# Two projection stages of a hybrid decoder block, ordered by hand, with the last two row blocks by column halves

## The chip, the cores and the metric

The kernel runs on one core of one Trainium2 chip. The metric is the device time of one execution in microseconds, as the median of several runs; a profiled execution gives the trace. The engines are PE (matmul, with its weight loads PEld beside it), DVE (vector), ACT (activation), POOL (GpSimd) and SP, which here only issues DMA.

## The reference

A decoder block (one layer, 256 rows of width 1024, fp32) with two parallel token mixers, a gated MLP and a final norm. Only its start concerns the change: the modulation from c, the norm, and the one wide input projection that feeds both mixers.

```python
cond = jax.nn.silu(c)
mod = (cond @ ada_w[layer] + ada_b[layer])[:, None, :]
shift_m, scale_m, gate_m, shift_f, scale_f, gate_f = jnp.split(mod, 6, axis=-1)
h = rmsnorm(x, norm_mix_g[layer]) * (1.0 + scale_m) + shift_m
...
p = split_columns(h @ w_in)   # q, k, v of the sparse attention, gates, latents, merge gates
...
o_nsa = lax.map(lambda a: nsa_one(*a, rel_table), (q, kc, vc, ks, vs, kw, vw, gates))
o_mla = mla_attention(p["mla_cq"], p["mla_ckv"], p["mla_krope"], ...)
y = jax.nn.sigmoid(p["merge_a"]) * o_nsa + jax.nn.sigmoid(p["merge_b"]) * o_mla
x = x + gate_m * (y @ w_o)
...
x = x + gate_f * conv_glu_ffn(h, ...)
return rmsnorm(x, final_norm_g)
```

Inside `nsa_one` every logit gets a bias from a small table by the distance of query and key.

## The kernel before

**Splitting.** Every fp32 operand is kept as two fp32r parts, hi and lo = value − hi. A product is three matmuls, hi·hi, hi·lo and lo·hi (`mm3`, L178). For a weight, ACT makes hi (L135) and DVE makes lo (L136) from the loaded tile `raw`. For the modulated input, tile by tile of 128 columns, DVE makes `hf` (L397), ACT its hi part `hh` (L398), DVE its lo part `hl` (L402).

**The start.** The transposed input xT comes in four loads on SP's queue; the parameters `par` and the identity (a part of `cst`) on ACT's. Eight matmuls broadcast silu(c) along the partitions into `crow`, which ACT copies out of PSUM (L300). Squares of xT (ACT, L304) are added up on DVE (L311) and reduced over partitions by matmuls with `ones` (L221); ACT and POOL make the inverse root, DVE scales the identity by it into `sq` (L268), and one matmul with ones broadcasts it (L272, `rsp`). `busy(n)` (L282) issues n matmuls of `ones` by `ones`, which compute nothing that is used; `WARM` holds how many stand at three places.

**Stage 1** (L410) multiplies eight row blocks k of `wA` (1024 × 2048), each in two column halves of eight tiles, into all eight PSUM banks: tags lg, lg, pt, pt, o, mm, mm, ms, called accA. A block is 48 matmuls of 128x256. The column of the modulation that block k + 1 needs is made meanwhile (`modulate`, L384): two rows of `adaA` are loaded, and DVE takes two dot products with `crow` (`gemv`, L377), then `am` (L393) and `mod` (L395).

**Stage 2** (L504) multiplies eight blocks of `wvg` (1024 × 560, 12 matmuls of 128x280 each) into the banks lg, lg, pt, pt, which must be emptied first: `t_evac` (L462 on ACT or L464 on DVE, as `TE` says) takes the lg banks, and `k_evac` the pt banks, as a copy on ACT (L478) and a subtraction on DVE (L479) from the same bank. `q_evac` (L448, L449) does the same for o, mm, mm, ms, which the attention's first logits need. At the end ACT copies v (L518) and the gates (L519) out.

**What sets the order.** A scheduler orders the instructions of each engine by the priorities of `prio` and by the code's order; `EV` orders the evacuations. `prefetch` keeps up to three weights loaded and split ahead. SP's queue takes the loads in the scheduler's order; each waits until the buffer it writes is free. The four loads of `BT` (L426, 512 KB each) read the table of biases from DRAM, shifted by partition. `tables` (L327) makes cosine and sine on DVE, from positions and the rest of `cst`.

**After stage 2** come the attention of both mixers with further projections between (list `WORK`), the output projection, the gated MLP and the last norm.

Of the kernel before, what the change touches and what calls it, by code (L numbers as in the profile page):

```python
# [14 lines left out]
AX = mybir.AxisListType  # L15

# [16 lines left out]
C_ID, C_MASK, C_VM, C_ROWV, C_IF, C_SGN = 0, 128, 512, 520, 521, 522  # L33
N_CST = 523

N_A = 16
WARM = (6, 3, 4)
# [3 lines left out]
HB = 3  # L41
# [5 lines left out]
EV = "k1 q1 t0 q3 q2 k0 d q0 t1"  # L47
# [3 lines left out]
TE = "avvvaaav"  # L51
# [4 lines left out]
def body(tc, a, out, dbg=None):  # L56
    nc = tc.nc
    with ExitStack() as ctx:
# [79 lines left out]

        depth = [3]
# [151 lines left out]
        acc = xsq[:, 0, :]  # L291
# [3 lines left out]
        with tc.issue_after(last[-1]):  # L295
            for c in range(2):
                ps = bank("pt")
                for i in range(4):
                    mm(ps[:, i * 128:i * 128 + 128], free(cond[:, 4 * c + i:4 * c + i + 1], [[0, 128]]), ident, True, True)
                nc.scalar.activation(crow[:, c * 512:c * 512 + 512], ps[:], AF.Copy)  # L300
        with tc.issue_after(silu), tc.issue_after(half):
            for i in range(4):
                sq = xsq.t[i // 2][:, i % 2 * 2:i % 2 * 2 + 2, :]
                nc.scalar.activation(sq, xT.t[i // 2][:, i % 2 * 2:i % 2 * 2 + 2, :], AF.Square)  # L304
                for j in range(2):
                    if i == 3 and j == 0:
                        ssq.reduce(acc, True, False)
                    if i == 3:
                        last.append(ssq.reduce(sq[:, j, :], False, j == 1))
                    elif i + j > 0:  # L310
                        nc.vector.tensor_tensor(acc, acc, sq[:, j, :], ALU.add)  # L311
# [15 lines left out]
        def tables():  # L327
# [6 lines left out]
            nc.sync.dma_start(cst[:, 128:], a["cst"][:, 128:])  # L334
# [47 lines left out]
        nc.vector.tensor_scalar(sb1[:], par[:, C_ADAB + 8:C_ADAB + 16], 1.0, None, ALU.add)  # L382

        def modulate(k):  # L384
            for j in (1, 0):
                if k % 3 < 2:
                    ad = l4(F32, [128, 1024])
                else:
                    ad = st.tile([128, 1024], F32, tag="ad", name=nm("ad"), bufs=2)
                nc.sync.dma_start(ad[:], a["adaA"][k, :, j])  # L390
                gemv(mod[:, 8 * j + k:8 * j + k + 1], ad[:])
# [3 lines left out]
            nc.vector.tensor_tensor(mod[:, k:k + 1], mod[:, k:k + 1], par[:, C_ADAB + k:C_ADAB + k + 1], ALU.add)  # L395
            hf = t1("hf")
            nc.vector.scalar_tensor_tensor(hf[:], xT[:, k, :], am[:], rst[:] if k else rsp, ALU.mult, ALU.mult)  # L397
            h0 = nc.scalar.activation(hh[:, k, :], hf[:], AF.Identity, bias=mod[:, k:k + 1]).ins  # L398
            if k == 0:
                with tc.issue_after(h0):  # L400
                    nc.scalar.activation(rst[:], rsp, AF.Copy)
            nc.vector.scalar_tensor_tensor(hl[:, k, :], hf[:], mod[:, k:k + 1], hh[:, k, :], ALU.add, ALU.subtract)  # L402

        modulate(0)
        nc.vector.tensor_scalar(vec[:], psv[0:16, 0:384], -1.0, None, ALU.mult)
        nc.gpsimd.dma_start(vdr[:], vec[:])
        prefetch(2)
        accA = [bank(t) for t in ("lg", "lg", "pt", "pt", "o", "mm", "mm", "ms")]
        prefetch(2)
        for k in range(8):  # L410
            if k < 7:
                modulate(k + 1)
            prefetch(3)
# [781 lines left out]
```

## Time and profile before

| | before |
|---|---|
| median of 3 runs | 456.95 us (456.25 to 459.64) |
| the profiled execution | 458.63 us, span 456.8 us |
| busy share of the span: PE, PEld | 96%, 91% |
| DVE, ACT, POOL | 80%, 62%, 6% |
| mean granted TensorE clock | 0.992 |

The span is the time from the first to the last instruction in the trace of one execution; the execution's own time lies 1.8 us above it. A busy share is the mean over stages with different limits, so the stages are looked at one by one. In a row of a timeline the bracket gives the idle time of the engine ahead of the instruction and what ended it; rows with "xN" hold N records that follow one another. Durations overlap where an engine is pipelined.

### The profile page before, as it was taken

The page shows a single profiled execution, that of the slowest core. Times are in us where ns is not written, and L with a number is a line of the kernel's source. Part 1 is how long each engine was busy: PE and PEld are TensorE (multiplying, and loading weights), DVE is VectorE, ACT ScalarE, POOL GpSimd, SP SyncE. Part 2 cuts the span into 40 slices and gives each one's busy share as a digit, 9 for nine tenths or more (in the row PEclk, how much of TensorE's full clock was granted, in tenths as well). Part 3 has the DMA queues.
Part 4 walks back from the last instruction along what each step waited for, and adds up shares of the span by engine and source line. Part 5 has one row for each costly group of instructions (what it writes and reads, how often), then busy time and mean ns, then how long its engine had stood idle before and what let it go on. Part 6 is the DMA issues. An engine that isn't in the chain of part 4 may idle for free.

```text
span 456.8 us, 9366 instructions
## 1 busy us (share of the span) xinstructions
PE 439.2 (96%) x3514; PEld 414.5 (91%) x3514; DVE 366.5 (80%) x873; ACT 282.3 (62%) x610; POOL 26.2 (6%) x45
## 2 busy tenths in 40 slices
PE   6999989999989999999999999999999999999994
PEld 6899978777869879999989999999999999999993
DVE  3899988878788878899989888778778778778643
ACT  4444475879698996656657776556556556546332
POOL 1100042030010111000000000000000000000001
PEclk9899999999999999999999999999999999999998
DMA  7999898779762337997857875655655655653002
GB/s 279 414 406 377 252 311 238 290 269 297 261 213 95 101 121 250 305 317 254 296 206 220 252 259 189 194 179 178 193 185 168 199 187 165 204 187 93 1 0 93
DMA packets 31565, 99.33 MB, mean 217 GB/s; under 512 B 4293, under 2 KB 6933, under 8 KB 31520
## 3 DMA queue, kind: packets, MB, share of 16 engines
q1 hardware_dynamic: 30208, 96.59, 62.7%
q0 software_dynamic: 1024, 1.98, 1.9%
q8 instruction: 28, 0.46, 0.4%
q10 hardware_dynamic: 288, 0.17, 0.2%
q14 instruction: 17, 0.14, 0.1%
HBM read 96.01 MB, written 1.14 MB: 213 GB/s over the span
## 4 chain that ended last, share of the span: by engine, by line
PE 79%; DVE 6%; DMA 6%; ACT 4%; issue 2%; POOL 1%; DVEq 0%; POOLq 0%; SPq 0%; ACTq 0%
PE mm L176 29%; PE lg L176 12%; PE o L176 12%; PE ms L176 11%; PE pt L176 10%; DMA ad<-in_adaR 3%; DMA cst<-in_cst 2%; PE pt L860 2%; DVE lo L136 2%; DVE ad L377 1%; ACT hi L135 1%; ACT pt L864 1%; PE ms L221 1%; ACT s L608 0%; DVE s L449 0%
## 5 line engine op out<-in xcount | busy, mean ns | idle before, releaser
L176 PE MATMUL mm<-s,hi 128*128 128x256 f32 x552 | 105.2, 288 | 0.6 <-DVE s L991 0.3
L136 DVE TENSOR_TENSOR s<-raw,s 128x1024 fp32r<-128x1024 f32 x66 | 80.5, 1221 | 17.9 <-PE mm L176 14.5
L176 PE MATMUL mm<-s,s 128*128 128x258 f32 (+1 forms) x544 | 94.1, 283 | 0.0
L176 PEld LDWEIGHTS mm<-s,hi 128*128 128x128 f32 x552 | 85.3, 189 | 3.7 <-issue 1.2
L135 ACT ACTIVATE s<-raw 128x1024 fp32r<-128x1024 f32 x66 | 69.0, 1051 | 23.2 <-PE mm L176 23.2
L176 PEld LDWEIGHTS mm<-s,s 128*128 128x128 f32 x544 | 77.6, 189 | 0.1
L176 PE MATMUL mm<-s,lo 128*128 128x256 f32 x268 | 76.9, 287 | 0.1
L136 DVE TENSOR_TENSOR lo<-raw,hi 128x1024 fp32r<-128x1024 f32 (+2 forms) x55 | 63.5, 1161 | 5.6 <-ACT hi L135 5.4
L135 ACT ACTIVATE hi<-raw 128x1024 fp32r<-128x1024 f32 (+2 forms) x55 | 53.5, 989 | 21.0 <-PE mm L176 6.8
L176 PEld LDWEIGHTS mm<-s,lo 128*128 128x128 f32 x268 | 50.5, 188 | 1.5 <-issue 0.7
L176 PE MATMUL o<-s,s 128*128 128x258 f32 (+1 forms) x272 | 47.8, 283 | 0.0
L377 DVE CUSTOM_DVE_ANT_0 ad<-ad,crow 128x1024 f32<-128x1024 f32 x36 | 43.6, 1218 | 3.2 <-DMA ad<-in_adaR 2.9
L176 PE MATMUL ms<-s,s 128*128 128x258 f32 x264 | 46.1, 283 | 0.0
L176 PEld LDWEIGHTS o<-s,s 128*128 128x128 f32 x272 | 39.0, 189 | 0.0
L176 PEld LDWEIGHTS ms<-s,s 128*128 128x128 f32 x264 | 37.7, 189 | 0.0
L176 PE MATMUL lg<-zh,s 128*128 128x256 f32 x176 | 34.7, 280 | 0.0
L176 PE MATMUL pt<-zh,s 128*128 128x256 f32 x176 | 34.6, 279 | 0.0
L839 ACT ACTIVATE L<-L,sm 128x128 f32<-128x128 f32 (+1 forms) x64 | 28.3, 449 | 1.4 <-DVE sm L835 1.4
L176 PEld LDWEIGHTS lg<-zh,s 128*128 128x128 f32 x176 | 28.6, 188 | 0.0
L176 PEld LDWEIGHTS pt<-zh,s 128*128 128x128 f32 x176 | 28.5, 188 | 0.0
L835 DVE CUSTOM_DVE_ANT_0 L<-lg,s 128x128 f32<-128x128 f32 (+1 forms) x64 | 20.9, 350 | 8.6 <-PE lg L176 8.0
L176 PE MATMUL lg<-s,s 128*128 128x256 f32 (+4 forms) x104 | 27.3, 350 | 0.5 <-DVE sm L835 0.5
(250 smaller groups left out, 810.4 us busy)
## 6 DMA issues: line engine op xcount, KB each, us to landing
ad<-in_adaR SPq DMA_DIRECT2D x32, 512.0 KB, 4.6
raw<-in_wg SPq DMA_DIRECT2D x22, 512.0 KB, 3.5
raw<-in_wu SPq DMA_DIRECT2D x22, 512.0 KB, 4.4
raw<-in_wd SPq DMA_DIRECT2D x22, 512.0 KB, 4.5
raw<-in_wA SPq DMA_DIRECT2D x16, 512.0 KB, 8.0
raw<-in_wm SPq DMA_DIRECT2D x16, 512.0 KB, 4.9
L<-in_adaA SPq DMA_DIRECT2D x12, 512.0 KB, 7.9
raw<-in_cw SPq DMA_DIRECT2D x8, 512.0 KB, 5.3
```

What stands on the lines that cost most here:

```text
L135: nc.scalar.activation(hi[:], raw[:], AF.Copy)
L136: nc.vector.tensor_tensor(lo[:], raw[:], hi[:], ALU.subtract)
L176: nc.tensor.matmul(o, l, r, start=start, stop=stop, **kw)
L221: m = nc.tensor.matmul(self.ps[:, tt:tt + 1], sq[:, tt * 128:tt * 128 + 128], ones[:, 0:1], start=first and tt == 0, stop=last, skip_group ...
L377: nc.vector.tensor_tensor_reduce(out=ad, in0=ad, in1=crow[:], scale=1.0, scalar=0.0, op0=ALU.mult, op1=ALU.add, accum_out=dst)
L835: nc.vector.tensor_tensor_reduce(out=L[:, br, j, 0:nk], in0=lgj[:, br, :], in1=bias_view(2 * t + j, qt), scale=1.0, scalar=3e38, op0=ALU.a ...
L839: nc.scalar.activation(L[:, br, j, 0:nk], L[:, br, j, 0:nk], AF.Exp, scale=-1.0, bias=sm[:, i:i + 1], accum_out=sm[:, 4 + i:5 + i])
L860: nc.tensor.transpose(pt[:, (kb * 2 + j) * 128:(kb * 2 + j) * 128 + 128], self.L[qt][:, br, j, kb * 128:kb * 128 + 128], ident)
L864: nc.scalar.activation(self.PT[qt, br][:, 0:qt + 1, :], pt[:, 0:(qt + 1) * 256].rearrange("p (b q) -> p b q", b=qt + 1), AF.Copy)
```

## The change

1. **Order by hand.** Stages 1 and 2, from the first `modulate` to the gates, stand in `tc.manual_schedule` for DVE, ACT and PE: these engines take them in the order of the code. `prefetch` is split for it into `fetch` (the load), `head` (hi) and `rest` (lo).
2. **Column halves.** The weights of `wA` come as before for blocks 0 to 5, then (6, half 0), (7, half 0), (6, half 1), (7, half 1). After the second of these the banks lg and pt are complete: `k_evac(1)`, `t_evac(0)`, `k_evac(0)` and `t_evac(1)` stand beside the other two, all eight copies of `t_evac` on ACT. `q_evac` is issued one half bank per block of stage 2. Stage 2 takes the row halves in the order 1, 0.
3. **The start.** The identity is a part of `par` and comes with it in one load on SP; xT comes in two loads on ACT's queue. DVE copies `crow`, ACT scales the identity, ACT makes `am` and `mod` and the negated `vec`; POOL prepares `sb1`. Each half of the squares is reduced by itself, and ones-matmuls stand at four places. Block 0 issues its products as all hi·hi, then hi·lo, then lo·hi.
4. **Around it.** `BT` is written behind stage 1; `tables` and the first later `gemv` wait for the gates' last instructions.

```diff
-WARM = (6, 3, 4)
+WARM = (5, 3, 3, 2)
-EV = "k1 q1 t0 q3 q2 k0 d q0 t1"
-TE = "avvvaaav"
+TE = "aaaaaaaa"
...
-        for k in range(8):
-            for c in range(2):
-                plan(a["wA"][k, :, c * (N_A // 2) * 128:(c + 1) * (N_A // 2) * 128], N_A // 2 * 128)
+        for k, c in [(k, c) for k in range(6) for c in range(2)] + [(6, 0), (7, 0), (6, 1), (7, 1)]:
+            plan(a["wA"][k, :, c * 1024:c * 1024 + 1024], 1024)
...
-        nc.scalar.dma_start(par[:], a["par"])
-        nc.scalar.dma_start(ident, a["cst"][:, C_ID:C_ID + 128])
-        for i in range(4):
-            nc.sync.dma_start(xT.t[i // 2][:, i % 2 * 2:i % 2 * 2 + 2, :], a["xT"][:, 2 * i:2 * i + 2, :])
+        ident = par[:, N_PAR:N_PAR + 128]
+        nc.sync.dma_start(par[:], a["par"])
+        for i in range(2):
+            nc.scalar.dma_start(xT.t[i][:], a["xT"][:, 4 * i:4 * i + 4, :])
...
+        for h in range(2):
+            t = xsq.t[h]
+            for j in range(2):
+                nc.vector.tensor_tensor(t[:, 2 * j, :], t[:, 2 * j, :], t[:, 2 * j + 1, :], ALU.add)
+            with tc.issue_after(last[-1]):
+                last.append(ssq.reduce(t[:, 0, :], h == 0, False))
+            with tc.issue_after(last[-1]):
+                last.append(ssq.reduce(t[:, 2, :], False, h == 1))
+            busy(WARM[2])
...
-            nc.vector.scalar_tensor_tensor(am[:], mod[:, 8 + k:9 + k], sb1[:, k:k + 1],
-                                           par[:, C_GMIX + k:C_GMIX + k + 1], ALU.add, ALU.mult)
+            nc.scalar.activation(am[:], mod[:, 8 + k:9 + k], AF.Identity, scale=par[:, C_GMIX + k:C_GMIX + k + 1],
+                                 bias=sb1[:, k:k + 1])
+            nc.scalar.activation(mod[:, k:k + 1], mod[:, k:k + 1], AF.Identity, bias=par[:, C_ADAB + k:C_ADAB + k + 1])
...
+        with tc.manual_schedule(engines={EN.DVE, EN.Activation, EN.PE}):
+            modulate(0, rsp)
+            head()
...
+            for k in range(8):
+                part_hi(k)
...
+                w = rest()
+                if k:
+                    part_lo(k)
+                head()
+                products(k, 0, w)
+                if k < 6:
+                    w = rest()
+                    head()
+                    products(k, 1, w)
+                if k < 7:
+                    modulate(k + 1, rst[:])
+
+            fetch()
+            w = rest()
+            head()
+            products(6, 1, w)
+            k_evac(1)
+            w = rest()
+            head()
+            fetch()
+            products(7, 1, w)
+            t_evac(0)
+            k_evac(0)
+            pending.append(rest())
+            head()
+            pending.append(rest())
+            t_evac(1)
...
+        queries = [(i, j) for i in (1, 3, 2, 0) for j in range(2)]
...
+                if k < 6:
+                    head()
+                    pending.append(rest())
+                i, j = queries.pop(0)
+                q_evac(i, (j,))
...
-        with prio("TB"):
+        with prio("TB"), tc.issue_after(ga), tc.issue_after(gv):
             tables()
...
-            gemv(mod[:, o + t:o + t + 1], ad[:])
+            with tc.issue_after(gv):
+                gemv(mod[:, o + t:o + t + 1], ad[:])
```

The first instructions of PE before, from the start of the program to the first product (`cond` is silu(c), `sq` the scaled identity, `o` receives the table of biases):

```order
L282 MATMUL lg_97<-ones 128x128 x6
L176 MATMUL pt_112<-cst,cond 128x128 x4
L176 MATMUL pt_118<-cst,cond 128x128 x4
L221 MATMUL ms_102<-ones,s_6_103 128x1 x2
L221 MATMUL ms_102<-ones,s_7_104 128x1 x4
L315 MATMUL o_140<-pt_85,tabx 16x384
L282 MATMUL lg_97<-ones 128x128 x3
L272 MATMUL ms_152<-sq_149,ones 128x256
L282 MATMUL lg_97<-ones 128x128 x4
L176 MATMUL lg_195<-s_16_161,hi_185 128x256
```

And after:

```order
L293 MATMUL lg_94<-ones 128x128 x5
L310 MATMUL pt_109<-par,cond 128x128 x4
L310 MATMUL pt_115<-par,cond 128x128 x4
L293 MATMUL lg_94<-ones 128x128 x3
L236 MATMUL ms_99<-ones,s_6_100 128x1 x4
L293 MATMUL lg_94<-ones 128x128 x3
L236 MATMUL ms_99<-ones,s_7_101 128x1 x4
L293 MATMUL lg_94<-ones 128x128 x3
L331 MATMUL o_102<-pt_82,tabx 16x384
L283 MATMUL ms_155<-sq_152,ones 128x256
L293 MATMUL lg_94<-ones 128x128 x2
L192 MATMUL lg_183<-s_16_162,hi_210 128x256 x2
```

Three ones-matmuls stand ahead of each half's four reductions and three behind the last; before, two and four reductions stood together. Block 0 begins with the hi parts alone.

SP's queue before, the first seven loads of `wvg` (`s` from `vdr` are the four BT loads):

```order
L116 DMA raw_714<-in_wvg 128x560
L116 DMA raw_744<-in_wvg 128x560
L426 DMA s_114_774<-vdr 128x4x256
L426 DMA s_115_775<-vdr 128x4x256
L426 DMA s_116_776<-vdr 128x4x256
L426 DMA s_117_777<-vdr 128x4x256
L116 DMA raw_840<-in_wvg 128x560
L116 DMA raw_858<-in_wvg 128x560
L116 DMA raw_876<-in_wvg 128x560
L116 DMA raw_894<-in_wvg 128x560
L116 DMA raw_912<-in_wvg 128x560
```

And after, from the first `cst` on (four loads of wvg stand before it):

```order
L348 DMA cst<-in_cst 128x395
L609 DMA ad_1150<-in_adaR 128x1024
L143 DMA raw_871<-in_wvg 128x560
L609 DMA ad_1153<-in_adaR 128x1024
L542 DMA s_124_811<-vdr 128x4x256
L542 DMA s_125_812<-vdr 128x4x256
L542 DMA s_126_813<-vdr 128x4x256
L542 DMA s_127_814<-vdr 128x4x256
L143 DMA raw_891<-in_wvg 128x560
L143 DMA raw_911<-in_wvg 128x560
```

The BT loads moved from ahead of the third block of wvg to behind the fifth (raw_871); `cst` and two rows of adaR (`ad`) stand ahead of them.

ACT before, at the border of the stages (lg, pt, mm, ms and o are PSUM banks; L478 is `k_evac`, L462 `t_evac`, L448 `q_evac`, L135 hi of a weight):

```order
L135 ACTIVATE hi_686<-raw_684 128x1024
L135 ACTIVATE hi_716<-raw_714 128x560
L135 ACTIVATE hi_746<-raw_744 128x560
L478 ACTIVATE s_122_786<-pt_198 64x2x256
L478 ACTIVATE s_122_786<-pt_197 64x2x256
L478 ACTIVATE s_123_787<-pt_198 64x2x256
L448 ACTIVATE s_119_783<-mm_200 64x2x256
L462 ACTIVATE s_126_790<-lg_195 64x2x128
L478 ACTIVATE s_123_787<-pt_197 64x2x256
L448 ACTIVATE s_121_785<-ms_202 64x2x256
L448 ACTIVATE s_120_784<-mm_201 64x2x256
L448 ACTIVATE s_119_783<-mm_200 64x2x256
```

And after (in the same order L477, L461, L447, L149):

```order
L149 ACTIVATE hi_696<-raw_588 128x1024
L149 ACTIVATE hi_726<-raw_655 128x1024
L477 ACTIVATE s_39_195<-pt_186 64x2x256
L477 ACTIVATE s_40_196<-pt_186 64x2x256
L149 ACTIVATE hi_758<-raw_723 128x560
L461 ACTIVATE s_43_199<-lg_183 64x2x128 x4
L477 ACTIVATE s_39_195<-pt_185 64x2x256
L477 ACTIVATE s_40_196<-pt_185 64x2x256
L149 ACTIVATE hi_799<-raw_761 128x560
L461 ACTIVATE s_44_200<-lg_184 64x2x128 x4
L149 ACTIVATE hi_845<-raw_831 128x560
L447 ACTIVATE s_36_192<-mm_188 64x2x256
```

The copies of the pt and lg banks come first, with hi of the next weights between, and those of mm behind them.

## Rows read from the trace of the kernel before

**Rows 1.** Windows: PE, PEld, DVE, ACT, POOL busy us (instructions); granted clock; DMA share; GB/s

```profile
9.00:12.00 3.00, 2.13 (x17) 1.88 (x17) 1.23 (x2) 1.27 (x3) 0.00 (x0) 1.00 1.03 408
13.00:16.00 3.00, 3.00 (x13) 2.78 (x13) 2.77 (x9) 0.96 (x2) 0.56 (x1) 0.50 1.02 416
17.40:62.60 45.20, 45.20 (x380) 45.13 (x380) 43.65 (x75) 19.76 (x26) 0.64 (x2) 1.00 0.97 358
62.60:78.70 16.10, 13.67 (x99) 12.71 (x98) 14.05 (x21) 11.23 (x25) 7.50 (x8) 1.00 0.91 226
...
130.00:140.00 10.00, 8.45 (x71) 6.67 (x71) 8.74 (x32) 9.95 (x33) 0.76 (x1) 1.00 0.45 154
```

**Rows 2.** Timeline of DVE, one row block of the first projection

```profile
35.60 1.22 DVE L377 CUSTOM_DVE_ANT_0 L<-L,crow 128x1024 f32<-128x1024 f32 x1
...
37.89 0.21 DVE L393 SCALAR_TENSOR_TENSOR am<-mod,sb,par 128x1 f32<-128x1 f32 x1
...
38.14 0.48 DVE L397 SCALAR_TENSOR_TENSOR hf<-s,am,rst 128x256 f32<-128x256 f32 x1
38.54 1.22 DVE L136 TENSOR_TENSOR lo<-raw,hi 128x1024 fp32r<-128x1024 f32 x1
39.68 0.48 DVE L402 SCALAR_TENSOR_TENSOR s<-hf,mod,s 128x256 fp32r<-128x256 f32 x1
40.16 1.22 DVE L136 TENSOR_TENSOR lo<-raw,hi 128x1024 fp32r<-128x1024 f32 x1
```

**Rows 3.** Timeline of PE at the border of the stages; idle time before in brackets

```profile
62.46 0.28 PE L176 MATMUL ms<-s,lo 128*128 128x256 f32 x1
63.49 0.50 PE L176 MATMUL pt<-hi,s 128*128 128x280 f32 x2 [0.75 <-DVE s L479]
...
65.42 0.50 PE L176 MATMUL lg<-hi,s 128*128 128x280 f32 x2 [0.92 <-DVE s L464]
...
75.57 0.42 PE L176 MATMUL lg<-hi,s 128*128 128x280 f32 x2
...
78.67 0.86 PE L176 MATMUL lg<-s,s 128*128 128x256 f32 x4
...
81.11 0.50 PE L176 MATMUL lg<-s,s 128*128 128x256 f32 x2 [0.51 <-DVE sm L835]
```

**Rows 4.** Chain of waits between 60 and 100 us: start, us, what

```profile
61.40 0.60 DVE s L479
62.02 0.60 ACT s L478
```

**Rows 5.** Timeline of the start, PE and ACT: the norm, the first weight, the first product

```profile
6.00 3.55 PE L176 MATMUL pt<-cst,cond 128*128 128x128 f32 x16 [2.01 <-DMA cst<-in_cst]
...
10.76 1.05 PE L221 MATMUL ms<-ones,s 128*128 128x1 f32 x8 [0.86 <-ACT s L304]
...
12.48 1.55 PE L282 MATMUL lg<-ones 128*128 128x128 f32 x6
...
12.53 1.06 ACT L135 ACTIVATE hi<-raw 128x1024 fp32r<-128x1024 f32 x1 [0.42 <-DMA raw<-in_wA]
...
13.83 1.17 PE L272 MATMUL ms<-sq,ones 128*128 128x256 f32 x2
...
15.62 0.51 ACT L398 ACTIVATE s<-hf,mod 128x256 fp32r<-128x256 f32 x1 [2.04 <-DVE mod L395]
```

**Rows 6.** Timeline of ACT in the second stage, three copies of t_evac

```profile
67.04 1.15 ACT L462 ACTIVATE s<-lg 64x256 f32<-64x256 f32 x3
```

**Rows 7.** Timeline of SP's queue before the second stage

```profile
51.56 2.42 SPq L426 DMA_DIRECT2D s<-vdr  x4
54.08 7.67 SPq L116 DMA_DIRECT2D raw<-in_wvg  x5
```

**Rows 8.** DMA issued between 54 and 54.5 us

```profile
DMA packets 143, 0.15 MB, mean 293 GB/s; under 512 B 0, under 2 KB 143, under 8 KB 143
...
raw<-in_wvg SPq DMA_DIRECT2D x1, 280.0 KB, 8.6
```

More of the change, by code (lines that the diff above doesn't have):

```diff
@@ L15 @@
 AX = mybir.AxisListType
+EN = mybir.EngineType
 S, D = 256, 1024
@@ L290, in body @@
         xsq = big(F32)
-        acc = xsq[:, 0, :]
+        psv = bank("o")
         busy(WARM[0])
         crow = cp.tile([128, 1024], F32, name="crow")
[L295 to L300, printed above, removed]
@@ L301, in body @@
-        with tc.issue_after(silu), tc.issue_after(half):
-            for i in range(4):
-                sq = xsq.t[i // 2][:, i % 2 * 2:i % 2 * 2 + 2, :]
-                nc.scalar.activation(sq, xT.t[i // 2][:, i % 2 * 2:i % 2 * 2 + 2, :], AF.Square)
-                for j in range(2):
[L306 to L311, printed above, removed]
+        for c in range(2):
+            ps = bank("pt")
+            for i in range(4):
+                with tc.issue_after(last[-1]):
+                    last.append(nc.tensor.matmul(ps[:, i * 128:i * 128 + 128],
+                                                 free(cond[:, 4 * c + i:4 * c + i + 1], [[0, 128]]), ident,
+                                                 start=True, stop=True).ins)
+            nc.vector.tensor_copy(crow[:, c * 512:c * 512 + 512], ps[:])
@@ new lines, in body @@
+        busy(WARM[1])
+        with tc.issue_after(silu):
+            for h in range(2):
+                for j in range(2):
+                    nc.scalar.activation(xsq.t[h][:, 2 * j:2 * j + 2, :], xT.t[h][:, 2 * j:2 * j + 2, :], AF.Square)
+        for h in range(2):
+            t = xsq.t[h]
[3 more added lines that the diff above has]
+                last.append(ssq.reduce(t[:, 0, :], h == 0, False))
+            with tc.issue_after(last[-1]):
+                last.append(ssq.reduce(t[:, 2, :], False, h == 1))
+            busy(WARM[2])
@@ L396, in modulate @@
[L396 to L404, printed above, removed]
@@ L423, in body @@
[L423 to L434 removed]
+                    ads[k, j] = st.tile([128, 1024], F32, tag="ad", name=nm("ad"), bufs=2)
@@ L439, in body, with part_hi, part_lo, q_evac @@
+        def part_hi(k):
+            nc.scalar.activation(hh[:, k, :], hfs[k][:], AF.Identity, bias=mod[:, k:k + 1])
+        def part_lo(k):
+            nc.vector.scalar_tensor_tensor(hl[:, k, :], hfs.pop(k)[:], mod[:, k:k + 1], hh[:, k, :], ALU.add, ALU.subtract)
+        fetch_ada(0)
+        fetch()
+        fetch()
+        fetch_ada(1)
+        fetch()
+        accA = [bank(t) for t in ("lg", "lg", "pt", "pt", "o", "mm", "mm", "ms")]
         QS = [s4(F32R) for _ in range(4)]
         KH, KL = [s4(F32R, (128, 2, 2, 256)) for _ in range(2)], [s4(F32R, (128, 2, 2, 256)) for _ in range(2)]
-        def q_evac(i):
-            for j in range(2):
+        def q_evac(i, js):
+            for j in js:
@@ new lines, in body, with bias_view, bias_view_c @@
+        BT = [[s4(F32) for _ in range(2)] for _ in range(2)]
+        vd = vdr[:]
+        for i in range(4):
+            nc.sync.dma_start(BT[i // 2][i % 2][:], bass.AP(tensor=vd.tensor, offset=vd.offset + i * 4 * 384,
+                                                              ap=[[1, 128], [384, 4], [1, 256]]))
+        def bias_view(h, qt):
+            b = BT[h // 8][h % 8 // 4][:, h % 4, :]
+            return free(b, [[-1, 256]], 255) if qt else free(b, [[-1, 128]], 127)
+        def bias_view_c(g, qt, n):
+            return free(BT[g // 2][g % 2][:, 0, :], [[256, 4], [-16, n]], 224 if qt else 96)
@@ L489, in proj @@
+        for gp in range(2):
+            for K in (KH, KL):
+                nc.gpsimd.dma_start(K[gp][64 - gp * 64:128 - gp * 64], K[gp][gp * 64:gp * 64 + 64])
         def proj():
```

151 lines of the change are left out of this document (77 added, 74 removed).

## The prediction

> **What bounds the kernel now.** I read the table of windows first, to see which engine is full in which stage [rows 1]. In the 45.20 us of the first projection PE is busy all 45.20 and DVE 43.65, so PE bounds it with DVE close behind; in the 16.10 us of the second stage PE is busy 13.67 only. So there is something to win at the start, in the second stage and just behind it, and little in the first.
>
> The DVE timeline gives the period of a row block [rows 2]: the gemvs begin at 35.60, the last lo at 40.16 takes 1.14 as the one before it did, and so the next pair comes at 41.30, 5.70 us later. PE needs the same, 48 matmuls at 45.20 / 380 = 0.119 us. With eight such blocks ending at 62.46 + 0.12 = 62.58, block 1 began, as if without a stall, at 62.58 − 7 × 5.70 = 22.7.
>
> The PE timeline behind 62.58 [rows 3] shows waits of 0.75 and 0.92 us on DVE evacuations (L479, L464). Where nothing waits, two blocks of the second stage take 78.67 − 75.57 = 3.10 us, eight 12.4; the stage took 78.67 − 62.58 = 16.09. So 3.7 us are lost there, and 0.51 more at 81.11 before the first softmax. The chain of waits [rows 4] shows why: ACT and DVE alternate on one bank, some 0.62 us a link. All of it together, 4.2 us, is the most that the border can give.
>
> **Part by part: the steady blocks.** Stage 1 keeps its 384 matmuls. am and mod (38.14 − 37.89 = 0.25 us of DVE a block [rows 2]) go to ACT, busy 19.76 of 45.20 us [rows 1], which hides them. DVE then needs 5.45 a block, PE still 5.70: term 0. If that cover were gone, the term would be the two instructions, 0.25 a block.
>
> **The start.** Before, the cond matmuls run 6.00 to 9.55 and the last reduction ends at 10.76 + 1.05 = 11.81 [rows 5]. In the new order three ones-matmuls stand ahead of each half's reduction. Three ones are six records, 1.55 us in [rows 5] at a granted clock of 0.50 [rows 1]; at the full clock I take half, 0.78 a group. (The cond matmuls' 3.55 us for 16 records would make it 1.33, +1.1 for both groups, kept as a bound.) A half's reduction is eight records, 1.05 by its row. From 9.4: 0.78 + 1.05 + 0.78 + 1.05 puts the end at 13.1. From there to the rsp matmul were 13.83 − 11.81 = 2.0 us, and ACT will need about as long with the identity: 15.1. On ACT am and mod follow (0.4, estimated from the 0.25 on DVE), then hi(0) 1.06, which before ran at 12.53, ahead of all this, then hh 0.51: 17.1, where before it ended at 16.13. On DVE follow hl 0.48, two lo at 1.14, two gemv 2.29, hf 0.40, lo 1.14, hl 0.48 = 7.07, plus 0.4 of waits: block 1 has its hl at 24.5 where its start stood at 22.7. I take **+1.6** (PE starts a block on hh, before it needs hl). Bounds: +0.6, if the ones vanish in gaps of PE, and +2.7, by the longer ones; the second rival goes beyond.
>
> **The column halves.** The order (6,0), (7,0), (6,1), (7,1) asks for hl(7) after half a block, 2.85 us of PE. DVE needs gemv 2.29, hf .40, lo 1.14, hl .48 = 4.31 for it, and the lead it has built by then (0.25 a block over five) is 1.25: **+0.2**, bounds 0 and +1.46.
>
> **The border.** Call E the end of (7,0). PE then has 2 × 2.85 + 12.4 = 18.1 us left in both stages, where before it was 5.70 + 16.09 = 21.8. But the new order brings waits. k_evac(1) has four alternating links of 0.62 [rows 4], to E + 2.7, and lo(7,1) 1.14 stands behind it on DVE: E + 3.9, where PE asks at E + 3.3. Then ACT has hi, four t_evac copies at 0.38 (three in 1.15 [rows 6]) and k_evac(0), which DVE follows by links; lo of the first wvg block stands behind those, at E + 7.35, and PE waits some 0.9 more. So 18.1 + 0.55 + 0.9 = 19.5, **−2.3**. Bounds: −3.7 if neither wait comes, 0 if waits like the old 0.75 and 0.92 double.
>
> **The bias transfers.** The order of SP's queue moves the four BT loads from ahead of the third wvg block to behind the fifth, and SP's row for the fifth waits for lo(7,1). Before, their issue took SP 2.42 us, and the wvg blocks issued from 54.08 on stood right behind them [rows 7]; the first landed 8.6 us after issue [rows 8], which 62.58 − 54.08 = 8.5 us of stage 1 hid. Now the issue falls on E + 4.9 to E + 7.3, and the sixth wvg block (wvg5) is issued at E + 7.4, lands at E + 16.0 if it also takes 8.6, and has hi 0.6 and lo 0.7 behind it. PE, at E + 7.15 + 5 × 1.55 = E + 14.9, wants it by then, its lo by E + 15.1: **+2.2**. Bounds: 0, if it flows as fast as the first stage's data do (first rival), and 3.5, if all its 3.2 MB (worked out below) go at the 293 GB/s of [rows 8]. I stay with 8.6, the row of the very same pair of transfers.
>
> **The entry of the attention.** PE's wait of 0.51 [rows 3] on DVE, which makes the tables then, goes, as the tables now come behind; late next is DVE, with a gemv and a cast now ahead of the first softmax, 1.2 us by [rows 2], covered in part by five bias-free matmuls of PE: **−0.5**, bounds −0.5 and +1.2. Behind it the scheduler shuffles instructions of the attention stage; PE idles 1.55 us there between 130 and 140 [rows 1], so I allow ±1.5 and take 0.
>
> **Sum:** 0 + 1.6 + 0.2 − 2.3 + 2.2 − 0.5 = +1.2. The profiled execution (458.63, span 456.8) would become 459.8. It lies 1.7 above the median of the three runs, 456.95, which is the better base, as the others are 456.25 and 459.64: 456.95 + 1.2 = **458.2**.
>
> **Rivals.** *First: the bias transfers flow as the rest does.* Between 9 and 16 us the DMA moved 408 to 416 GB/s [rows 1]. At E + 4.9 there stand ahead of and with wvg5 one wvg (0.29 MB), one row of adaR (0.52), BT (2.1) and itself (0.29): 3.2 MB, 7.7 us at 416, which is E + 12.6; with 1.5 us for landing and 1.3 for hi and lo it comes at E + 15.4, and the wait is 0.3, not 2.2: 458.2 − 1.9 = 456.3; with the start at its lower bound, +0.6, it is 455.3. For it: the second stage, with less to move, had 226 GB/s [rows 1] and so room. Against it: beside BT, in packets of some 1 KB, the queue moved 293 GB/s [rows 8]. The Trainium skill ("DMA: Bandwidth & Descriptors", section "Queues, rings and completion order") says that an issuing engine's transfers use rings on the same sixteen engines and are taken up in ring order; the 8.6 us agree with that. Its section "Where 436 GB/s comes from" puts the ceiling at 435 GB/s; as an estimate by that page BT alone would take 4.8 us, and the sum would go with this rival.
>
> *Second, the slower side: PE at half clock before the rsp matmul.* In 13 to 16 us the granted clock was 0.50, 1.2 instead of 2.4 GHz; in 9 to 12 it was 1.00 with PE busy 2.13 of 3.00 us [rows 1]. If it fell by 9.4 in the new order, the added ones and reductions would take twice 3.66 us: reductions end at 16.8, +3.7, all on the path: 458.2 + 3.7 = 461.9. It decides if the granted clock in 9 to 13 us is under 0.8. For it: the fall came before 13 us, behind PE's gap of 0.86 before 10.76 [rows 5]. Against it: the ones fill just that gap. The Trainium skill ("TensorE: Matmul & The Clock Gate", Part 1) says that the throttled state is the default and activity releases it; by that rule the ones hold the full clock through the rsp matmul (1.17 us in [rows 5], at 0.50), some 0.6 less, 457.6. The trace agrees in direction: the clock is 1.00 right behind the cond matmuls.
>
> *Third: the scheduled part of the change does as it says with no new waits,* border −3.7, transfers 0, start +0.6, halves +0.2, entry −0.5: −3.4, 453.6.
>
> **Chances.** The forecast 0.50, the first rival 0.25, the second 0.13, the third 0.12. About 1%, 4.6 us (452.4 and 461.5), is what a measurement of this kernel can tell from no change. All waits that could go (4.2) don't reach it without help from the attention stage, so faster gets 0.08, from the third rival and a lucky shuffle; slower 0.13 is the second rival and the far end of the start; same 0.79. The range goes from just above the third rival, 453.8, to just under the second, 461.3; what lies outside is some 0.2.
>
> **What would show it.** Right: the sixth block of stage 2 preceded by a PE wait of about 2 us on hi or lo of wvg, whose transfer landed over 8 us after issue; hh of block 0 some 1 us later than 15.62; waits of 0.75 and 0.92 at the border gone, with two of 0.5 to 0.9 in their place; stage 1's end followed by 13.8 us to the end of stage 2, without the DMA wait. Wrong: a stage 2 without a DMA wait (first or third rival); a granted clock under 0.8 between 9 and 13 us (second); a block of stage 1 over 5.8 us (the term 0); over 1.5 us gone or gained behind 90 us.

## The result, and the profile after

| | before | after |
|---|---|---|
| median of 4 runs each | 458.29 us (456.25 to 459.86) | 471.64 us (470.62 to 475.99) |
| ratio, 95% interval | | 1.031 (1.023 to 1.039) |
| profiled execution, span | 458.63, 456.8 us | 471.67, 469.8 us |
| first `hh` of ACT begins | 15.62 | 16.60 |
| first product behind stage 2 | 78.67 | 89.33 |
| from there to the end of the span | 378.1 | 380.5 |

The kernel became 3.1% slower where 458.2 us, no change, was forecast. The forecast was 1.2 us above 456.95, the median of before's first three runs; with a fourth that median is 458.29. The span grew by 13.0 us: 1.0 ahead of the first `hh`, 9.7 from there to the end of stage 2, 2.4 (378.1 to 380.5) behind it.

Busy time on the page of after; PE's share fell from 96% to 94%:

```profile
PE 442.2 (94%) x3524; PEld 416.0 (89%) x3524; DVE 363.3 (77%) x850; ACT 290.1 (62%) x631; POOL 25.6 (5%) x47
```

The windows of after, columns as in [rows 1]. The first two answer to the rows of the start, the rest is what became of the 16.10 us of stage 2:

```profile
9.00:12.00 3.00, 3.00 (x20) 3.00 (x20) 2.80 (x6) 0.61 (x2) 0.00 (x0) 1.00 1.03 415
13.00:16.00 3.00, 2.65 (x17) 1.77 (x17) 0.00 (x0) 1.79 (x6) 0.71 (x1) 1.00 1.02 410
...
64.00:70.00 6.00, 4.66 (x38) 4.46 (x37) 4.88 (x6) 4.65 (x9) 5.41 (x7) 1.00 1.01 271
70.00:74.00 4.00, 4.00 (x33) 4.00 (x32) 3.48 (x5) 1.86 (x3) 1.26 (x2) 1.00 1.17 222
74.00:78.00 4.00, 0.86 (x7) 0.64 (x5) 0.00 (x0) 0.00 (x0) 0.00 (x0) 1.00 1.22 245
78.00:82.00 4.00, 0.00 (x0) 0.00 (x0) 0.00 (x0) 0.00 (x0) 0.00 (x0) 0.66 1.08 373
...
84.00:86.00 2.00, 2.00 (x10) 2.00 (x10) 1.91 (x4) 1.45 (x4) 0.00 (x0) 0.50 0.71 217
```

From 78 to 82 us no engine of the row does anything, and the DMA engines are full. Then PE works at a granted clock of 0.50. The timeline of PE's waits at the border, which answers to [rows 3], and the first product behind the stage:

```profile
62.92 0.39 PE L192 MATMUL o<-s,lo 128*128 128x256 f32 x1 [0.67 <-DVE lo L153]
67.12 0.40 PE L192 MATMUL pt<-lo,s 128*128 128x280 f32 x1 [1.34 <-DVE lo L153]
82.89 0.83 PE L192 MATMUL pt<-hi,s 128*128 128x280 f32 x2 [8.03 <-ACT hi L149]
...
89.33 1.57 PE L192 MATMUL ms<-raw,s 128*64 128x256 f32 x10
```

The waits of 0.75 and 0.92 on evacuations are gone and two on `lo` stand in their place, both as forecast. The third is the loss. The chain of waits says what it is (start, us, what):

```profile
67.13 14.94 DMA raw<-in_wvg
...
82.17 0.68 ACT hi L149
...
82.89 2.08 PE pt L192 x6
84.97 1.34 PE lg L192 x6
86.31 0.77 PE pt L192 x6
87.08 0.78 PE lg L192 x6
```

The sixth block of `wvg` was issued at 67.13, right behind BT (SP's queue below), and took 14.94 us. The block that waited for it then took 3.42 us at half clock where the next takes 1.55: 8.0 of waiting and 1.9 of clock.

```profile
63.84 2.69 SPq L542 DMA_DIRECT2D s<-vdr  x4
67.13 5.14 SPq L143 DMA_DIRECT2D raw<-in_wvg  x3
```

DMAs issued by after between 64 and 67 us, then between 67 and 70 (KB each, median us to landing), then the queues' moves between 70 and 74 (q1 is SP's queue, q0 POOL's; packets, MB, share of the 16 engines):

```profile
s<-vdr SPq DMA_DIRECT2D x4, 512.0 KB, 14.0
s<-s POOLq DMA_DIRECT2D x2, 256.0 KB, 8.6
...
raw<-in_wvg SPq DMA_DIRECT2D x1, 280.0 KB, 14.9
...
q1 hardware_dynamic: 477, 0.48, 65.6%
q0 software_dynamic: 127, 0.40, 49.1%
```

Here stands what the prediction had not looked at. `s<-s` on POOL's queue are the four copies of K's halves (256 KB each, from SBUF to SBUF), which are issued as soon as `k_evac` is done. While they run, SP's queue moves 0.48 MB in 4 us, 120 GB/s, where it had moved 293 beside BT before [rows 8]. POOL's timeline of before and then of after shows that they themselves moved far less than BT (the first and the last of four):

```profile
61.88 0.53 POOL L485 DMA_DIRECT2D s<-s  x1 [47.89 <-ACT s L478]
...
66.67 0.55 POOL L485 DMA_DIRECT2D s<-s  x1
```

```profile
64.53 0.56 POOL L554 DMA_DIRECT2D s<-s  x1
...
70.73 0.53 POOL L554 DMA_DIRECT2D s<-s  x1
```

Before, BT was issued at 51.56 and the first of the copies ten us later. In after the four copies stand 2.7 to 4.5 us later and BT 12.3: BT came to them.

### The profile page after: what moved, and what is told of

Same layout as the page of the kernel before. It is cut to its first block, busy times and chain, and to the rows that moved or that the text cites. A ratio compares the mean times of both kernels' runs of the same rounds, so it can differ in the third digit from the quotient of the medians.

```text
span 469.8 us, 9387 instructions
## 1 busy us (share of the span) xinstructions
PE 442.2 (94%) x3524; PEld 416.0 (89%) x3524; DVE 363.3 (77%) x850; ACT 290.1 (62%) x631; POOL 25.6 (5%) x47
## 4 chain that ended last, share of the span: by engine, by line
PE 75%; DVE 7%; DMA 7%; ACT 6%; issue 3%; POOL 1%; SPq 0%; POOLq 0%; DVEq 0%; ACTq 0%
PE mm L192 30%; PE o L192 11%; PE lg L192 11%; PE ms L192 10%; PE pt L192 8%; DMA raw<-in_wvg 3%; PE pt L937 2%; DMA ad<-in_adaR 2%; DVE lo L153 2%; ACT hi L149 2%; DVE L L391 1%; DVE ad L391 1%; DMA par<-in_par 1%; PE ms L236 1%; PE pt L310 1%
## 5 line engine op out<-in xcount | busy, mean ns | idle before, releaser
L135 DVE TENSOR_TENSOR s<-raw,s 128x1024 fp32r<-128x1024 f32 x66 | 80.5, 1221 | 17.8 <-PE mm L192 14.8
L134 ACT ACTIVATE hi<-raw 128x1024 fp32r<-128x1024 f32 (+1 forms) x31 | 32.4, 1044 | 15.4 <-PE mm L192 6.5
L135 DVE TENSOR_TENSOR lo<-raw,hi 128x1024 fp32r<-128x1024 f32 (+1 forms) x31 | 37.1, 1201 | 3.7 <-ACT hi L134 3.7
L153 DVE TENSOR_TENSOR lo<-raw,hi 128x1024 fp32r<-128x1024 f32 (+1 forms) x24 | 26.9, 1124 | 10.2 <-ACT hi L149 9.7
L149 ACT ACTIVATE hi<-raw 128x1024 fp32r<-128x1024 f32 (+1 forms) x24 | 21.9, 923 | 12.3 <-DMA raw<-in_wvg 10.0
```

The source lines that it names most:

```text
L134: nc.scalar.activation(hi[:], raw[:], AF.Copy)
L135: nc.vector.tensor_tensor(lo[:], raw[:], hi[:], ALU.subtract)
L149: nc.scalar.activation(raws[0][1][:], raw[:], AF.Copy)
L153: nc.vector.tensor_tensor(lo[:], raw[:], hi[:], ALU.subtract)
```

## The experiments

All runs stand in one table. Column three is the time from the first `hh` to the first product behind stage 2, which leaves out how the start went; the fourth is the rest of the span. These three come from one profiled execution of each kernel, the median from all of its runs, so they need not add up to it. Before was run again with each group of runs, hence its range of medians.

| kernel | `hh` at | `hh` to end of stage 2 | rest | median, us |
|---|---|---|---|---|
| before | 15.62 | 63.05 | 378.1 | 458.3 to 459.5 |
| after | 16.60 | 72.73 | 380.5 | 471.64 |
| e1 BT early | 15.98 | 62.86 | 388.7 | 468.08 |
| e2 no K copies | 17.39 | 65.10 | 380.7 | 465.01 (1 run) |
| e3 no BT | 17.15 | 62.76 | 383.7 | 465.33 (1 run) |
| e4 before, BT late | 15.31 | 73.89 | 384.8 | 475.82 (1 run) |
| e5 e1, attention's weights held | 20.08 | 62.87 | 383.9 | 465.13 |
| e6 own queue for wvg | 16.36 | 68.78 | 382.7 | 469.65 (1 run) |
| e7 e5 without ones | 16.98 | 62.85 | 384.8 | 466.79 |
| e8 before, gated | 16.45 | 63.03 | 381.8 | 463.04 (1 run) |
| e9 after, not gated | 20.32 | 72.91 | 380.8 | 475.79 (1 run) |
| e10 e5, cst and tables early | 16.88 | 68.80 | 380.2 | 471.07 |
| e11 nothing ahead of wvg | 15.76 | 62.87 | 386.2 | 465.76 |
| e12 before again | 15.68 | 63.05 | 377.9 | 458.42 (1 run) |

Theory: BT beside the K copies delays the sixth block of `wvg`. Rivals: BT alone does it by its size; the order of SP's ring does it; the hand order's own chains do it.

### e1: BT early

```diff
+            BT = [[s4(F32) for _ in range(2)] for _ in range(2)]
+            for i in range(4):
+                nc.sync.dma_start(BT[i // 2][i % 2][:], ...)
             fetch()
             w = rest()
             head()
             products(6, 1, w)
...
-        BT = ... (the same four loads, behind stage 1)
```

> Issues the four BT loads in the changed kernel where the kernel before had them in SP's queue, ahead of the third wvg block; cst and two rows of adaR fall behind wvg by the scheduler's own choice. Theory A (BT stands ahead of wvg5 in SP's queue and shares the DMA with the K copies of POOL's queue): the wait of 8.0 us ahead of the sixth block of stage 2 and the half clock behind it go, some 9.9 us, so about 461.5 us. Theory B (the K copies alone hold wvg5 up, wherever BT stands): the wait stays over 4 us, over 466. Theory C (the loss is in the order by hand, the DMA only its sign): wvg5 comes early but another wait of that size takes its place, over 468.

Measured: 468.08 us, ratio 1.020 (1.012 to 1.027). Stage 2 has no DMA wait; `wvg` landed in 4.4 us and the K copies in 4.6. From `hh` to the end of the stage it takes 62.86, 9.9 less than after. But a new wait of 4.13 stands behind it, PE's row and the row of ACT that leads to it:

```profile
80.74 1.06 ACT L134 ACTIVATE hi<-raw 128x1024 fp32r<-128x1024 f32 x1 [3.47 <-DMA raw<-in_wc]
```

```profile
83.68 0.51 PE L192 MATMUL lg<-s,s 128*128 128x256 f32 x2 [4.13 <-ACT gate L595]
```

The scheduler had put a `hi` of the attention's weights ahead of the last copies of `gate`, and ACT stood 3.47 us for its transfer. The rest of the span took 388.7, which gave back most of the gain. So theory A's wait went, as it says, and its time (461.5) did not come; theory C's time came, with a wait half as long as it asks for, behind the stage and not in it. e5 below takes that wait away.

### e2 and e3: without the K copies, without BT

In e2, and in e3:

```diff
+        for gp in range(2):
+            for K in (KH, KL):
+                nc.gpsimd.memset(K[gp][64 - gp * 64:128 - gp * 64].bitcast(F32), 0.0)
...
-                nc.gpsimd.dma_start(K[gp][64 - gp * 64:128 - gp * 64], K[gp][gp * 64:gp * 64 + 64])
```

```diff
+            nc.gpsimd.memset(BT[i // 2][i % 2][:], 0.0)
...
-            nc.sync.dma_start(BT[i // 2][i % 2][:], ...)
```

The zeroing stands ahead of stage 1.

> Leaves out the four copies of K's halves within SBUF on POOL's queue; the halves are set to zero early, so half of the attention's first logits lack that part. BT stays where the change put it. Theory A: BT's loads land some 7 to 8 us after issue instead of 14.0, wvg5 some 8 to 9 after issue instead of 14.9, and the wait ahead of the sixth block is 1.5 to 3 us, about 464 us, as my forecast had it. If BT alone makes the loss: landing and wait stay at 14 and 8 us, 471.

> Leaves out the four BT loads; BT is set to zero early by POOL, so the logits have no bias. The K copies stay. Theory A: wvg5 lands 4 us or less after issue, no wait ahead of the sixth block, about 461 us. Theory B: wvg5 still lands over 8 us after issue and PE waits over 2 us.

The two things each by itself: DMAs of e2 issued between 60 and 70 us, its PE wait, and the copies among the DMAs of e3 issued between 60 and 74:

```profile
s<-vdr SPq DMA_DIRECT2D x4, 512.0 KB, 7.9
...
raw<-in_wvg SPq DMA_DIRECT2D x3, 280.0 KB, 7.3
```

```profile
77.13 0.52 PE L192 MATMUL pt<-hi,s 128*128 128x280 f32 x2 [1.97 <-ACT hi L149]
```

```profile
s<-s POOLq DMA_DIRECT2D x4, 256.0 KB, 4.6
```

Without the copies BT lands in 7.9 instead of 14.0, the sixth block in 8.4 instead of 14.9, and the wait is 1.97, close to the 2.2 of the prediction's transfer term. Without BT the copies land in 4.6 instead of 8.6, and no block of stage 2 waits for a transfer. Either alone costs 2.2 or nothing (65.10 and 62.76 against 62.87), both together 9.9. So it is the pair, and BT's size alone is not the cause. In time e2 came near its forecast (465.01, 464 forecast) and e3 did not (465.33, 461 forecast): there PE waits 3.11 us for the gates at the entry of the attention, behind a `hi` as in e1.

### e4: the same in the kernel before

```diff
+                    kl.append(nc.vector.tensor_tensor(KL[gp][rows, :, br, :], ps, ...).ins)
...
+            if e == "q1":
+                for i in range(4):
+                    with tc.issue_after(kl[0]), tc.high_priority(offset=400):
+                        nc.sync.dma_start(BT[i // 2][i % 2][:], ...)
```

> The kernel before, with only the BT loads moved behind the seventh wvg block and behind the first K evacuation, so that they meet the K copies on POOL's queue. Theory A: BT lands over 11 us after issue (7.4 before), wvg7 behind it over 10, PE waits 1 to 4 us for the last block: 458 to 462 us. If BT's landing has nothing to do with the K copies: 7 to 8 us, wvg7 in time, 457.

Measured: 475.82 us, where 458 to 462 was forecast. DMAs issued between 61 and 75 us, then DVE and PE:

```profile
s<-vdr SPq DMA_DIRECT2D x4, 512.0 KB, 12.6
s<-s POOLq DMA_DIRECT2D x4, 256.0 KB, 9.0
...
mg<-in_pos SPq DMA_DIRECT2D x2, 8.0 KB, 10.0
```

```profile
78.62 0.20 DVE L337 CAST mg<-mg 128x64 f32<-128x64 int32 x1 [9.33 <-DMA mg<-in_pos]
```

```profile
80.37 0.83 PE L176 MATMUL lg<-lo,s 128*128 128x280 f32 x2 [10.14 <-DVE lo L136]
```

The transfers do what theory A says, in a kernel without the hand order: BT lands in 12.6 us instead of 7.4, the copies in 9.0 instead of 6.2, and the eighth `wvg` block, issued behind BT at 64.48, in 13.7. The wait of 10.14, though, is not for that block. The scheduler has the first instruction of `tables` on DVE ahead of three `lo` of `wvg`, and the positions that it reads stand behind BT in SP's ring: 8 KB that take 10.0 us. So from `hh` to the end of stage 2 it is 10.8 us longer than before through the place of BT and without the hand order, but by another chain than in after. That the two losses are near in size (10.8 and 9.9) does not make them one.

### e6: the last blocks of wvg on a queue of their own

```diff
-                if k < 6:
-                    fetch()
+                if k == 0:
+                    for _ in range(3):
+                        fetch()
+                if k < 3:
+                    fetch(nc.scalar)
```

`fetch(q)` issues on queue q; the `hi` of the attention's weights is held as in e5.

> The changed kernel with BT and the K copies where the change put them, but the last three wvg blocks loaded by ACT's queue instead of standing behind BT on SP's (and the pin of e5). Theory A in its form 'order in SP's rings': wvg5 lands under 7 us after issue, no wait over 1 us in stage 2, about 461 to 464 us. If the bytes themselves are too many for the time (BT, K copies and wvg together): wvg5 lands 10 us or more after issue and a wait of over 3 us stays.

Measured: 469.65 us, a wait of 3.75 and its half-clock block. DMAs issued between 66 and 71 us:

```profile
raw<-in_wvg ACTq DMA_DIRECT2D x3, 280.0 KB, 10.7
s<-s POOLq DMA_DIRECT2D x3, 256.0 KB, 8.7
```

The block, issued at 66.92 and off BT's ring, still takes 10.7 us, where the blocks took 3.2 in e3 without BT. Of after's 9.9 us, 5.9 are left (68.78 against 62.87). So, by one run, standing behind BT in the ring is 4 us of the loss, and the shared engines the larger part.

### e5 and e7: the attention's weights held; without the ones

e5 is e1 with `hi` and `lo` of the attention's first weights held behind the gates, and e7 is e5 with the second edit:

```diff
+                    with tc.issue_after(gated[0]) if gated else nullcontext():
                         nc.scalar.activation(hi[:], raw[:], AF.Copy)
+                    with tc.issue_after(gated[1]) if gated else nullcontext():
                         nc.vector.tensor_tensor(lo[:], raw[:], hi[:], ALU.subtract)
...
+        gated += [ga, gv]
```

```diff
-WARM = (5, 3, 3, 2)
+WARM = (5, 0, 0, 2)
```

> As e1, and the hi and lo parts of the attention's first weights are issued only behind the gates' last instructions, so that a hi that waits for its DMA can't stand ahead of ACT's last copies. If the 4.1 us that PE waited for those copies in e1 were a side effect of that one instruction: the wait goes, stage 2 ends within 0.5 us of before (78.67), about 464 us. If the entry needs that time anyway: another wait of 3 us or more before the first softmax, 467 or more.

> As e5, without the ones-matmuls around the reductions (WARM 5, 0, 0, 2). My term of the start: the reductions end 1.5 to 2 us earlier than 13.35 and hh of block 0 comes 0.8 to 2 us earlier, block 1 of stage 1 likewise: 462 to 463 if e5 is 464. Second rival turned round (the clock needs the ones): the rsp matmul takes over 1 us at a granted clock near 0.50 and the gain is under 0.5.

e5: 465.13 us, ratio 1.013 (1.009 to 1.017); the wait at the entry fell from 4.13 to 0.56, yet the rest of the span takes 383.9. Its profiled execution shows a start that after's did not have, PE's timeline and a window in it:

```profile
10.67 1.71 PE L238 MATMUL ms<-ones,s 128*128 128x1 f32 x8
...
13.66 1.71 PE L238 MATMUL ms<-ones,s 128*128 128x1 f32 x8
...
18.17 1.22 PE L285 MATMUL ms<-sq,ones 128*128 128x256 f32 x2
```

```profile
12.00:15.00 3.00, 3.00 (x15) 3.00 (x16) 1.35 (x4) 0.00 (x0) 0.00 (x0) 1.00 1.03 415
```

In after the same rows are:

```profile
10.65 1.13 PE L236 MATMUL ms<-ones,s 128*128 128x1 f32 x8
11.65 0.91 PE L293 MATMUL lg<-ones 128*128 128x128 f32 x6
12.40 0.95 PE L236 MATMUL ms<-ones,s 128*128 128x1 f32 x8
...
15.21 0.70 PE L283 MATMUL ms<-sq,ones 128*128 128x256 f32 x2 [0.34 <-ACT sq L281]
```

Records that take 0.95 and 0.70 there take 1.71 and 1.22 here, and `hh` comes 3.5 us later, though the window's granted clock says 1.00. This profiled execution took 468.64 us, the longest of e5's five.

e7: 466.79 us, 1.018 (1.014 to 1.021), no gain:

```profile
9.79 3.41 PE L238 MATMUL ms<-ones,s 128*128 128x1 f32 x16
15.07 1.22 PE L285 MATMUL ms<-sq,ones 128*128 128x256 f32 x2 [0.48 <-ACT sq L283]
```

Without the ones the sixteen reductions take 0.21 a record and end at 13.2; in after, with them, 0.12, and they end at 13.35. Counted from the start of the cond matmuls, `hh` begins after 10.8 us in both: what the ones take the reductions give back. That holds while the records behind them run at the faster rate. In e5, with ones and the slower rate, `hh` begins after 14.3, 3.5 us later than without ones.

### e8 to e11: the rest of the span, and a better order

e8 is the kernel before with the change's gating alone, e9 is after without it:

```diff
-        with prio("TB"), tc.issue_after(ga), tc.issue_after(gv):
+        with prio("TB"):
             tables()
...
-            with tc.issue_after(gv):
-                gemv(mod[:, o + t:o + t + 1], ad[:])
+            gemv(mod[:, o + t:o + t + 1], ad[:])
```

e10 is e5 with the loads of positions and `cst` ahead of BT (`table_loads`) and `tables` behind the last `lo` of stage 2. e11 is e10 with two column writes that hold the first loads of `adaR` behind the last block of `wvg`:

```diff
+            table_loads()
             BT = [[s4(F32) for _ in range(2)] for _ in range(2)]
...
-        with prio("TB"), tc.issue_after(ga), tc.issue_after(gv):
+        with prio("TB"), tc.issue_after(last_lo):
             tables()
```

```diff
+                    if k == 5:
+                        ads = [st.tile([128, 1024], F32, tag="ad", ...) for _ in range(2)]
+                        for ad in ads:
+                            nc.vector.tensor_copy(ad[:, 0:1], mod[:, 0:1])
```

> The kernel before with one edit of the change alone: the tables and the first later gemv wait for the gates' last instructions. If the 2.4 us that the changed kernel lost behind stage 2 come from this edit: 458.5 to 460, with PE's idle time behind 130 us grown. If not: within 1 us of before, the wait of 0.51 at the entry smaller.

> The changed kernel without one of its edits: tables and the first later gemv no longer wait for the gates; the scheduler puts them on DVE ahead of q_evac in stage 2. BT and the K copies stay, so the wait for wvg5 stays (7 to 9 us). If the gating costs what e8 seemed to show: from the end of stage 2 to the end of the span some 377 to 379 us instead of 380.6, in all 467 to 470. If that stretch differs from run to run and order to order for other reasons: 380 or more, 470 or more.

> Everything the runs showed against the change put right at once: BT and the loads for the tables ahead of the third wvg block, the pin of e5, and the tables on DVE right behind the last lo of stage 2 instead of behind the gates. Stage 2 without a DMA wait should end at 78.5 to 79.5 us (if PE's clock rises at the start as in the changed kernel's profile), and the rest should take 378 to 381: 456.5 to 460.5 in all, no better than the kernel before, since the start's 1.0 us eats the border's gain. If the hand order costs more than DMA and entry: over 462.

> The kernel after with the four bias loads and the loads of positions and cst behind stage 1's weights, the tables freed after the last lo of the second stage, the hi of the attention's weights after the gates, and the first two rows of adaR loaded only behind the seventh and eighth block of wvg, so that no bulk but POOL's copies of K runs beside the wvg blocks. Theory (the loss is bulk ahead of wvg on engines that the K copies share): wvg lands in under 7 us, no PE wait over 1.5 us on hi or lo of a wvg block or on the gates, stage 2 ends 20 to 21 us after the end of stage 1's second half block, so by 79 to 80.5 us, and the time is 459 to 464. Rival (the hand order itself is slower by its chains, the transfers only come on top): PE still waits 2 us or more in stage 2 with data landed, and the time stays over 465.

e8 has a rest of 381.8, 3.7 more than before, and e9 one of 380.8, as long as after. So gating can cost the kernel before something, but it is not what costs after its 2.4. That reading failed. In e9 the one wait of 7 to 9 us that was forecast came as three, of 3.65, 1.97 and 1.67 us, with `tables` between the `lo` on DVE; the stage is as long as in after (72.91 against 72.73). e10 (471.07 us, 1.027, 1.022 to 1.032) has `adaR` ahead of the sixth `wvg` block instead of BT, and waits 3.64 us: a megabyte of another load there does it too. e11 has none there; `wvg` and the K copies land in 4.8 and 4.2, and no block waits for a transfer. Its stage 2 ends at 78.63, a little earlier than the theory's 79 to 80.5. But the time is 465.76 us, 1.012 (1.006 to 1.017), over the 464 I had expected; the rival's time came without the rival's waits in stage 2. The rest takes 386.2, with a wait of 1.74 (PE at 212.62, for DVE) and behind it again 3 us at half clock:

```profile
214.00:217.00 3.00, 3.00 (x13) 2.70 (x12) 2.15 (x7) 0.84 (x4) 0.00 (x0) 0.50 0.77 243
```

### e12: before again

> The kernel before unchanged, a second profile of it. If the 2.4 us that the kernel after took longer behind the second stage belong to its order, this profile has its rest within 1 us of 378.1 us; if they are what one profile differs from the next by, it lies at 379 us or more. hh of block 0 within 0.9 us of 15.62, as the other profiles of this start.

458.42 us; `hh` at 15.68, rest 377.9, within 0.2 of the first profile. So the 2.4 us behind stage 2 in after, of which there is one profile, are twelve times what the two of before differ by, and I take them as its order's. PE's waits from the end of stage 2 on (us in total, times, longest), of before and then of after, the three longest of each:

```profile
PE o L176 <- ACT pt L864: 0.8, 1, 0.8
PE o L176 <- DVE mg L955: 0.6, 1, 0.6
PE o L176 <- ACT Pc L750: 0.6, 1, 0.6
```

```profile
PE o L192 <- ACT pt L941: 1.3, 1, 1.3
PE o L192 <- DVE mg L1032: 1.1, 1, 1.1
PE mm L192 <- ACT s L1034: 1.0, 1, 1.0
```

All such waits together are 3.6 us in before and 5.7 in after: 2.1 of the 2.4. They lie in the attention and behind it. Which moved instruction brings each was not found.

## Why the prediction was wrong, point by point

**The steady blocks: right.** Behind the start, PE's waits in stage 1 add up to the 0.55 and 0.24 us named below, and to no others over 0.2. Term 0.

**The start: right, in after's profile.** Predicted: reductions end at 13.1, the rsp matmul at 15.1, `hh` ends at 17.1. Measured: 13.35, 15.21, 17.11. PE's wait for block 1's `hl` (0.55) puts that block at 24.23, predicted 24.5. The end of (7, 0), E, is 58.76, predicted 56.88 + 1.6 + 0.2 = 58.7. The wait for `hl(7)` is 0.24, predicted 0.2.

**The border: right in kind, half in size.** The waits behind `lo(7,1)` and the first `wvg` block's `lo` came where they were forecast, 0.67 and 1.34 instead of 0.55 and 0.9. From E to the end of stage 2 are 30.57 us, 20.7 without the 9.9, where the prediction had 19.5 and before 21.8: −1.1 instead of −2.3. The two waits are 0.56 of the 1.2 that are missing; the rest was not traced.

**The bias transfers: the step that failed.** "I stay with 8.6, the row of the very same pair of transfers." The pair took 14.9. The issue came at E + 8.4 (predicted 7.4), and PE wanted the data at E + 16.1 (predicted 14.9), so these two nearly cancel. PE stood from 74.86 on (82.89 − 8.03), the data came at 82.07, and the term measured +9.9 instead of +2.2, far over its upper bound of 3.5. The row was of the same two transfers but not of the same company: from 54 to 58 us only SP's queue ran, at 67 us the K copies did, too. The prediction asked how long SP's queue would be and never what POOL's queue moves at that time, though both timelines were there to lay side by side. e2 takes the copies away and measures 8.4 for the landing, 2.0 of wait and 2.2 of loss, the very number of the term; e4 puts BT beside the copies in the kernel before, and BT takes 12.6 there instead of 7.4. The 1.9 us at half clock are a second thing that the term lacked: it priced a wait as the wait alone. Taken out of the kernel, the 9.9 come back only in part: e5 is 6.7 us and e11 6.3 above before's median of the same group of runs, where after is 13.4 above, since the rest grows from 380.5 to 383.9 and 386.2.

The Trainium skill ("DMA: Bandwidth & Descriptors", section "Queues, rings and completion order") also says that each DMA engine takes its queues in turn, packet by packet; the trace agrees in that both queues were on the engines in one stretch (65.6% for SP's queue and 49.1% for POOL's between 70 and 74 us), and the turn itself no row shows. Had it been laid beside the K copies, BT's slowing would have been on the list. What the prediction drew from that section, the ring's order, explains 4 of the 9.9 us (e6).

**The rivals.** The first (transfers flow at 416 GB/s) fell: even without the copies BT took 7.9 us. Its 1.5 us for landing stood in no row; loads of 8 KB took 2.0 in after, ahead of BT. The second (half clock ahead of the rsp matmul) did not decide this result, but a start at half the rate exists: two of the nine profiles with the ones in this order (e5, e9) have `hh` at 20.1 and 20.3, 3.5 to 3.7 later than after, close to the 3.7 that the rival had priced. Its test, a granted clock under 0.8 between 9 and 13 us, would have missed it; the durations show it, and whether the clock made them is open. The Trainium skill ("TensorE: Matmul & The Clock Gate", Part 1) says that activity releases the throttle, by which the ones hold the clock: with them the rsp matmul took 0.70 us in after, without them 1.22 (e7), which agrees, and e5, with the ones and 1.22, does not. The third rival (no new waits) fell with the transfers and with the two new waits on `lo`, which stay where the DMA waits go (0.95 and 1.09 in e1). e1, e5, e7 and e11 show what is won without the DMA waits: `hh` to the end of stage 2 takes 62.85 to 62.87 us against 63.05 in before. The hand order of both stages is worth 0.2 us of the 3.7 that the prediction found lost there, since what the border wins (1.1) is mostly spent between `hh` and E (42.2 us against 41.3).

**The entry and the rest: wrong in sign.** The 0.51 at the first softmax went, as said; yet from the end of stage 2 on 2.4 us came in all, where the prediction had −0.5, outside the ±1.5 that I allowed.

**The sum.** +1.0 ahead of `hh`, −0.2 from `hh` to the end of stage 2, +9.9 the transfer with its clock, +2.4 behind: 13.1, where the spans differ by 13.0.

No version here beats the kernel before. The best two, e11 and e5, are 1.2% and 1.3% slower. e11's loss lies behind stage 2; in e5's profile 5.8 us lie there and 4.5 at the start. What lengthens the rest is open.

## What to carry to other kernels

When a bulk transfer is moved, lay every queue's issues beside its new place, also the on-chip copies that another engine issues there; a landing time taken from a row holds only in the company that the row had. Ask also which small loads then stand behind the bulk in its ring, and who waits for them. Price a wait of many microseconds with the half-clock work that follows it. An order set by hand for one stage is judged with what the scheduler does behind it: here the stage came out even and the loss stood later.

## What the runs showed of the hardware

- Copies from SBUF to SBUF on POOL's queue and loads on SP's queue slowed each other: BT took 7.9 us without the copies (e2) and the copies 4.6 without BT (e3), 14.0 and 8.6 together, more for BT than the 12.5 of one after the other. The DMA engines then showed shares of 1.17 and 1.22 and moved 222 and 245 GB/s in all, against 410 and 415 at a share of 1.02 and 1.03 in the start of after.
- A small load stood behind a large one on its queue: 8 KB of positions took 2.0 us ahead of BT (after) and 10.0 behind it (e4). On ACT's queue the blocks behind BT took 10.7 us instead of 14.9 (e6).
- After 8.0 us without a matmul the granted clock was 0.50 for some 3 us of work (0.50 between 82 and 86 us, 0.98 between 86 and 89), and a block took 3.42 us instead of 1.55. In e11, 1.74 us of waiting had 3 us at 0.50 behind them as well, from 1.4 us after their end on; in e2, 1.97 us of waiting had none (1.00 from 77.1 to 80 us).
- In the first 20 us the clock's row can mislead: reductions of 8 records took 1.71 us (e5) or 0.95 (after) with 1.00 in both rows. In e8 it read 0.50 from 9 to 16 us, and 8 records took 1.87.
